# A softmax over rows of 512: transfers merged into one queue, the Tile context closed early, ScalarE in loops

## The chip, the core and the metric

The kernel runs on one core of one Trainium2 chip. The metric is device time in microseconds (us) of one execution; the profile, taken in an execution of its own, gives a span from the first to the last instruction and what every engine and every DMA queue did in it. Engines are called DVE (VectorE), ACT (ScalarE), POOL (GpSimd), PE (TensorE, unused here) and SP (SyncE). The 16 DMA engines move data between HBM and the on-chip memory; instructions issue transfers into queues, here the hardware queue of SP (q1 in the profile) and that of ACT (q10).

## The reference

```python
x = np.random.randn(16, 1024, 512).astype(np.float32)

def reference(x):
    x_max = np.max(x, axis=-1, keepdims=True)
    exp_x = np.exp(x - x_max)
    return (exp_x / np.sum(exp_x, axis=-1, keepdims=True)).astype(np.float32)
```

A softmax along the last axis: 16384 rows of 512 float32 values, 33.55 MB in and 33.55 MB out.

## The kernel before

The 16384 rows are cut into 8 chunks of 2048 rows. A chunk lies on 128 partitions with 16 rows on each (`CHUNK`), so a partition's part of a chunk is 32 KB that are contiguous in HBM too, and a chunk is 4.19 MB. The on-chip tile `held` has room for 6 chunks (`PLACES`); chunk k uses place k mod 6, and everything is computed in place. Chunks 6 and 7 therefore can be loaded only when chunks 0 and 1 have been stored.

The computation goes by groups of 8 rows a partition (`GROUP`), two groups to a chunk, 16 groups in all. For a group:

- `rowmax` (line 89): one DVE instruction gives the negated maximum of each row, `shift`.
- `exps` (line 94): eight ACT activations, one for each row of a partition, give exp(x + shift) in place; each also accumulates the row's sum into `sums`, which appears in the profile as a separate ACTIVATION_READ_ACCUMULATOR.
- `scale` (line 105): one small DVE instruction gives the reciprocals of the eight sums. Then, for groups 0 to 12 (`ON_POOL = 13`), one POOL instruction (line 107) multiplies the whole group of 4096 elements a partition with the reciprocals, which are broadcast along the row; for groups 13 to 15 eight DVE instructions (line 114) do it, one for each row.

The order on each engine is the program's order (`manual_schedule`): DVE does the maximum of group g ahead of the reciprocal of group g - 1. The Tile context supplies the semaphores between engines.

All loads are issued by SP (line 72): six at once at the beginning, the first of them ahead of the opening barrier of the program (`loads_at_the_head`). All stores are issued by ACT (line 75), between its activations; `STORE_BEHIND` says how many groups later a finished chunk's store stands in ACT's order. The loads of chunks 6 and 7 follow the stores of chunks 0 and 1 in the program; SP waits for those stores to land. So loads are in SP's queue and stores in ACT's.

When the Tile context ends (line 161), SP waits for every transfer and every engine's last instruction; then two barriers of all engines follow, with a clearing of the context's semaphores between them.

Of the kernel before, what the change touches and what calls it, by code (L numbers as in the profile page):

```python
# [1 line left out]

# [4 lines left out]

F32 = mybir.dt.float32
EXP = mybir.ActivationFunctionType.Exp
AX = mybir.AxisListType.X  # L10


CHUNK = 16
CHUNKS = 8
PLACES = 6
GROUP = 8

STORE_BEHIND = [1, 1, 1, 1, 0, 0, 0, 0]

LOAD_AFTER = {0: 6, 1: 7}  # L20
ON_POOL = 13


AT_HEAD = {mybir.EngineType.SP: 1}

def loads_at_the_head(nc):

    main, body = nc.main_func.blocks[0], nc.main_func.blocks[1]  # L30
    for engine, count in AT_HEAD.items():
        loads = [
            i
            for i in body.instructions
            if i.engine == engine and type(i).__name__ == "InstDMACopy"
        ][:count]
        barrier = next(
            n
            for n, i in enumerate(main.instructions)
            if i.engine == engine and type(i).__name__ == "InstDrain"  # L40
        )
        for load in loads:
            body.instructions.remove(load)
        main.instructions[barrier:barrier] = loads


@with_exitstack
def kernel(
    ctx: ExitStack,
    tc: tile.TileContext,  # L50
    x: bass.AP,
    out: bass.AP,
):
    nc = tc.nc
    nc.at_finalize(loads_at_the_head)
    P = nc.NUM_PARTITIONS

    x_rows = x.flatten_outer_dims().rearrange("(c p r) d -> c p r d", p=P, r=CHUNK)
    out_rows = out.flatten_outer_dims().rearrange("(c p r) d -> c p r d", p=P, r=CHUNK)
    n, _, _, d = x_rows.shape  # L60
    assert n == CHUNKS

    data = ctx.enter_context(tc.tile_pool(name="data", bufs=1))
    stats = ctx.enter_context(tc.tile_pool(name="stats", bufs=6))
    held = data.tile([P, PLACES * CHUNK, d], F32, name="held")

    def place(k):
        at = (k % PLACES) * CHUNK
        return held[:, at : at + CHUNK, :]

    def load(k):
        nc.sync.dma_start(out=place(k), in_=x_rows[k])  # L72

    def store(k):
        nc.scalar.dma_start(out=out_rows[k], in_=place(k))
        if k in LOAD_AFTER:
            load(LOAD_AFTER[k])

    per = CHUNK // GROUP
    groups = CHUNKS * per  # L80
    shift, sums = [None] * groups, [None] * groups

    def rows(g):
        at = (g % per) * GROUP
        return place(g // per)[:, at : at + GROUP, :]

    def rowmax(g):
        shift[g] = stats.tile([P, GROUP], F32, name="shift", tag="shift")
        nc.vector.reduce_max(out=shift[g], in_=rows(g), axis=AX, negate=True)  # L89

    def exps(g):
        sums[g] = stats.tile([P, GROUP], F32, name="sums", tag="sums")
        for r in range(GROUP):
            nc.scalar.activation(  # L94
                out=rows(g)[:, r, :],
                in_=rows(g)[:, r, :],
                func=EXP,
                bias=shift[g][:, r : r + 1],
                scale=1.0,
                accum_out=sums[g][:, r : r + 1],  # L100
            )

    def scale(g):
        recip = stats.tile([P, GROUP], F32, name="recip", tag="recip")
        nc.vector.reciprocal(out=recip, in_=sums[g])  # L105
        if g < ON_POOL:
            nc.gpsimd.tensor_mul(  # L107
                out=rows(g),
                in0=rows(g),
                in1=recip.unsqueeze(2).to_broadcast([P, GROUP, d]),  # L110
            )
            return
        for r in range(GROUP):
            nc.vector.tensor_scalar_mul(  # L114
                out=rows(g)[:, r, :],
                in0=rows(g)[:, r, :],
                scalar1=recip[:, r : r + 1],
            )

    with tc.manual_schedule():  # L120
        for k in range(PLACES):
            load(k)
        stored = 0
        for g in range(groups):
            rowmax(g)
            exps(g)
            if g:
                scale(g - 1)
            if stored < CHUNKS and g > (stored + 1) * per - 1 + STORE_BEHIND[stored]:
                store(stored)  # L130
                stored += 1
        scale(groups - 1)
        while stored < CHUNKS:
            store(stored)
            stored += 1


# [1 line left out]
_INS = ['x']  # L139
_OUTS = [((16, 1024, 512), 'float32')]  # L140


# [23 lines left out]
```

## Time and profile before

| What | Value |
|---|---|
| time, median of 3 runs | 161.96 us (161.58 to 162.31) |
| span of the profiled execution | 160.4 us |
| DVE, ACT, POOL busy | 51%, 58%, 57% of the span |
| DMA | 67.13 MB, mean 419 GB/s |

The profiled execution has no other time than its span. The median of the runs is 1.55 us longer than that span: the runs' time also holds what lies ahead of the first and behind the last instruction of the program.

How the views are read. The page's first rows give the busy time of each engine, its share and the number of instructions; the row "DMA" cuts the span into 40 slices and gives the mean busy share of the 16 DMA engines in tenths. The chain of waits follows the work that ended last backwards from one releaser to the next; its rows are start, duration, what. Groups of instructions give line, engine, operation, shapes and count, then busy time and mean duration in ns, then the idle time ahead of them and what ended it. The view by stretches gives, for each stretch, its length, the busy time and the number of instructions of DVE, ACT and POOL, the granted TensorE clock, the busy share of the DMA engines, and GB/s; bytes are counted where their packet begins. In the timeline an engine's name with a q (ACTq, SPq) is its sequencer: issues, waits and drains, which are not counted as busy.

### The profile page before, as it was taken

Reading aid. Unit: us, or ns where it says so; the run is one execution under the profiler, and the core shown is the slowest. Engines: PE = TensorE matmul, PEld = TensorE weight load, DVE = VectorE, ACT = ScalarE, POOL = GpSimd, SP = SyncE. Lnnn points to the kernel's source line nnn. Section 1 sums busy time; section 2 is a strip of 40 time slices with the busy share of each in tenths; the row PEclk is TensorE's granted clock in tenths of the full one; section 3 lists DMA queues with packets and bytes.
Section 4 is the critical chain, followed back from the end, with each engine's and each line's share of the span. In section 5 each row is a group of like instructions: output and inputs, shape, how many; then the busy total and the mean of one; then the engine's idle time right before and its main releaser. Section 6 shows DMA issues by size and latency. Waiting matters only on the chain.

```text
span 160.4 us, 425 instructions
## 1 busy us (share of the span) xinstructions
DVE 82.0 (51%) x56; ACT 92.7 (58%) x257; POOL 91.0 (57%) x17
## 2 busy tenths in 40 slices
DVE  0009967977977700893009920099202999671000
ACT  0003899999998996079900959409594195920000
POOL 0000039999999999999993899508995000000000
DMA  7999999999899999999999999999999999999993
GB/s 261 482 433 392 466 449 392 443 458 400 343 433 400 449 449 409 425 474 409 425 466 409 409 490 409 402 466 441 400 449 449 409 425 474 411 409 474 425 392 139
DMA packets 2307, 67.13 MB, mean 419 GB/s; under 512 B 256, under 2 KB 256, under 8 KB 256
## 3 DMA queue, kind: packets, MB, share of 16 engines
q1 hardware_dynamic: 1152, 33.55, 49.5%
q10 hardware_dynamic: 1152, 33.55, 48.5%
q14 instruction: 3, 0.02, 0.0%
HBM read 33.55 MB, written 33.55 MB: 418 GB/s over the span
## 4 chain that ended last, share of the span: by engine, by line
DMA 53%; POOL 14%; DVE 10%; ACT 7%; issue 7%; DVEq 0%; SPq 0%
DMA held<-in_x_dram 34%; DMA out_dram<-held 19%; POOL held L107 14%; ACT held L94 7%; DVE shift L89 6%; DVE held L114 4%; DVE recip L105 0%; DVEq L161 0%; SPq L72 0%; DVEq L105 0%; DVEq L89 0%
## 5 line engine op out<-in xcount | busy, mean ns | idle before, releaser
L94 ACT ACTIVATE held<-held,shift 128x512 f32<-128x512 f32 x128 | 90.6, 719 | 36.4 <-DVE shift L89 32.0
L107 POOL TENSOR_TENSOR held<-held,recip 128x4096 f32<-128x4096 f32 x13 | 90.8, 7018 | 31.5 <-DVE recip L105 31.5
L89 DVE TENSOR_REDUCE shift<-held 128x8 f32<-128x4096 f32 x16 | 70.2, 4393 | 46.9 <-DMA held<-in_x_dram 46.9
L94 ACT ACTIVATION_READ_ACCUMULATOR held<-held,shift 128x1 f32 x128 | 25.3, 198 | 0.0
L105 DVE RECIPROCAL recip<-sums 128x8 f32<-128x8 f32 x16 | 3.2, 200 | 16.0 <-ACT held L94 16.0
L114 DVE TENSOR_SCALAR held<-held,recip 128x512 f32<-128x512 f32 x24 | 9.8, 483 | 0.1
L94 ACT ACT_TABLE_LOAD x1 | 1.3, 1283 | 12.3 <-DMA held<-in_x_dram 12.3
L150 POOL MEMSET const-float32-0.0<- 128x1 f32 x1 | 0.1, 99 | 0.2 <-issue 0.2
L150 POOL MEMSET const-bfloat16-1.0<- 128x1 bf16 x1 | 0.1, 102 | 0.0
L150 POOL MEMSET const-uint8-127<- 128x1 uint8 x1 | 0.1, 102 | 0.0
L150 POOL MEMSET const-float32-1.0<- 128x1 f32 x1 | 0.1, 99 | 0.0
## 6 DMA issues: line engine op xcount, KB each, us to landing
held<-in_x_dram SPq DMA_DIRECT2D x8, 4096.0 KB, 41.8
out_dram<-held ACTq DMA_DIRECT2D x8, 4096.0 KB, 28.0
```

What stands on the lines that cost most here:

```text
L89: nc.vector.reduce_max(out=shift[g], in_=rows(g), axis=AX, negate=True)
L94: nc.scalar.activation(out=rows(g)[:, r, :], in_=rows(g)[:, r, :], func=EXP, bias=shift[g][:, r : r + 1], scale=1.0, accum_out=sums[g][:, ...
L105: nc.vector.reciprocal(out=recip, in_=sums[g])
L107: nc.gpsimd.tensor_mul(out=rows(g), in0=rows(g), in1=recip.unsqueeze(2).to_broadcast([P, GROUP, d]),)
L114: nc.vector.tensor_scalar_mul(out=rows(g)[:, r, :], in0=rows(g)[:, r, :], scalar1=recip[:, r : r + 1],)
L150: nc = _bacc.Bacc("TRN2", target_bir_lowering=False, num_devices=1)
```

## The change

The kernel after computes the same values in the same chunks and groups. What is different:

- **Own memory and semaphores.** `held`, `shift`, `sums` and `recip` are allocated directly, the three statistics with a place for every row, and the kernel declares its own semaphores: one for each load, one for each store, one for each chunk's finished multiplications, and four between the engines. `take` waits until a semaphore has reached n and lowers it by n.
- **Tile context closed early.** Only the six first loads stand in the context. It is closed behind them, so its closing barriers come right after the loads' issue. Nothing of the kind stands at the end; there SP waits for the six stores that no load has waited for.
- **One queue.** Stores are issued by SP too. After the six loads SP's order is: store 0, store 1, load 6, store 2, load 7, store 3 to 7, each store behind the wait for its chunk's two multiplications, loads 6 and 7 behind the landing of stores 0 and 1.
- **ScalarE in loops.** ACT loads its function table at once. Its 16 groups run in two loops, of 12 and of 4 turns, with eight activations in the body; the addresses of the rows and of the statistics are computed from the loop's counter in registers, by two instructions ahead of each activation.
- **Multiplications.** Groups 0 to 11 are multiplied on POOL as before, groups 12 to 15 on DVE (`ON_VECTOR`), there with the same single instruction with broadcast reciprocals in place of eight. Group 12 thus moves from POOL to DVE.
- The order on DVE is as before, with waits of its own: the maximum of a chunk's first group waits for its load, the reciprocal for ACT's group. The first POOL instruction that sets up the multiplication stands behind POOL's first wait; before, it stood ahead of it.

```diff
+ORDER = [("L", k) for k in range(PLACES)] + [
+    ("S", 0), ("S", 1), ("L", 6), ("S", 2), ("L", 7),
+    ("S", 3), ("S", 4), ("S", 5), ("S", 6), ("S", 7),
+]
+ON_VECTOR = (12, 13, 14, 15)
...
+    def take(engine, semaphore, n):
+        engine.wait_ge(semaphore, n).then_inc(semaphore, -n)
...
-    def load(k):
-        nc.sync.dma_start(out=place(k), in_=x_rows[k])
-
-    def store(k):
-        nc.scalar.dma_start(out=out_rows[k], in_=place(k))
-        if k in LOAD_AFTER:
-            load(LOAD_AFTER[k])
...
+    with tc.manual_schedule():
+        for _, k in ORDER[:PLACES]:
+            first = nc.sync.dma_start(out=place(k), in_=x_rows[k])
+            first.then_inc(loaded[k], 16)
+            tc.no_tile_sem_insts.add(first.ins.name)
+    tc.close()
+    tc.compile()
+
+    reused = set()
+    for what, k in ORDER[PLACES:]:
+        if what == "L":
+            if k >= PLACES:
+                take(nc.sync, stored[k - PLACES], 16)
+                reused.add(k - PLACES)
+            nc.sync.dma_start(out=place(k), in_=x_rows[k]).then_inc(loaded[k], 16)
+        else:
+            take(nc.sync, scaled[k], PER)
+            nc.sync.dma_start(out=out_rows[k], in_=place(k)).then_inc(stored[k], 16)
...
     def rowmax(g):
+        if g % PER == 0:
+            take(nc.vector, loaded[g // PER], 16)
+        nc.vector.reduce_max(
+            out=stats(shift, g), in_=rows(g), axis=AX, negate=True
+        ).then_inc(maxed, 1)
 
     def scale(g):
-        nc.vector.reciprocal(out=recip, in_=sums[g])
-        if g < ON_POOL:
-            nc.gpsimd.tensor_mul(...)
-            return
-        for r in range(GROUP):
-            nc.vector.tensor_scalar_mul(...)
+        engine, ready = (
+            (nc.vector, to_vector) if g in ON_VECTOR else (nc.gpsimd, to_pool)
+        )
+        take(nc.vector, expd, 1)
+        nc.vector.reciprocal(out=stats(recip, g), in_=stats(sums, g)).then_inc(ready, 1)
+        take(engine, ready, 1)
+        engine.tensor_mul(
+            out=rows(g),
+            in0=rows(g),
+            in1=stats(recip, g).unsqueeze(2).to_broadcast([P, GROUP, d]),
+        ).then_inc(scaled[g // PER], 1)
...
+    nc.scalar.preload_act_table(EXP)
+
+    def exps(first, turns):
+        with nc.scalar.Fori(0, turns) as i:
+            take(nc.scalar, maxed, 1)
+            for r in range(GROUP):
+                row = held[:, bass.ds(i * GROUP + r, 1), :]
+                at = bass.ds(i * GROUP + (first * GROUP + r), 1)
+                act = nc.scalar.activation(
+                    out=row, in_=row, func=EXP, bias=shift[:, at],
+                    scale=1.0, accum_out=sums[:, at],
+                )
+            act.then_inc(expd, 1)
+
+    exps(0, RING)
+    exps(RING, GROUPS - RING)
+
+    for k in range(CHUNKS):
+        if k not in reused:
+            take(nc.sync, stored[k], 16)
```

More of the change, by code (lines that the diff above doesn't have):

```diff
@@ L61 @@
     assert n == CHUNKS
-    data = ctx.enter_context(tc.tile_pool(name="data", bufs=1))
-    stats = ctx.enter_context(tc.tile_pool(name="stats", bufs=6))
-    held = data.tile([P, PLACES * CHUNK, d], F32, name="held")
+    held = nc.alloc_sbuf_tensor("held", [P, PLACES * CHUNK, d], F32).ap()
+    shift = nc.alloc_sbuf_tensor("shift", [P, GROUPS * GROUP], F32).ap()
+    sums = nc.alloc_sbuf_tensor("sums", [P, GROUPS * GROUP], F32).ap()
+    recip = nc.alloc_sbuf_tensor("recip", [P, GROUPS * GROUP], F32).ap()
+    loaded = [nc.alloc_semaphore(f"loaded{k}") for k in range(CHUNKS)]
+    stored = [nc.alloc_semaphore(f"stored{k}") for k in range(CHUNKS)]
+    maxed = nc.alloc_semaphore("maxed")
+    expd = nc.alloc_semaphore("expd")
+    to_pool = nc.alloc_semaphore("to_pool")
+    to_vector = nc.alloc_semaphore("to_vector")
+    scaled = [nc.alloc_semaphore(f"scaled{k}") for k in range(CHUNKS)]
+    def take(engine, semaphore, n):
+        engine.wait_ge(semaphore, n).then_inc(semaphore, -n)
     def place(k):
@@ L69, in place @@
         return held[:, at : at + CHUNK, :]
-    def load(k):
-        nc.sync.dma_start(out=place(k), in_=x_rows[k])
-    def store(k):
-        nc.scalar.dma_start(out=out_rows[k], in_=place(k))
-        if k in LOAD_AFTER:
-            load(LOAD_AFTER[k])
-    per = CHUNK // GROUP
-    groups = CHUNKS * per
-    shift, sums = [None] * groups, [None] * groups
-    def rows(g):
-        at = (g % per) * GROUP
-        return place(g // per)[:, at : at + GROUP, :]
-    def rowmax(g):
-        shift[g] = stats.tile([P, GROUP], F32, name="shift", tag="shift")
-        nc.vector.reduce_max(out=shift[g], in_=rows(g), axis=AX, negate=True)
@@ L91, in exps @@
-    def exps(g):
-        sums[g] = stats.tile([P, GROUP], F32, name="sums", tag="sums")
-        for r in range(GROUP):
[L94 to L101, printed above, removed]
-    def scale(g):
-        recip = stats.tile([P, GROUP], F32, name="recip", tag="recip")
-        nc.vector.reciprocal(out=recip, in_=sums[g])
-        if g < ON_POOL:
[L107 to L111, printed above, removed]
-            return
[L113 to L135, printed above, removed]
+    def rows(g):
+        at = (g % RING) * GROUP
+        return held[:, at : at + GROUP, :]
@@ new lines, in stats @@
+    def stats(t, g):
+        return t[:, g * GROUP : (g + 1) * GROUP]
+    with tc.manual_schedule():
[15 more added lines that the diff above has]
+            nc.sync.dma_start(out=out_rows[k], in_=place(k)).then_inc(stored[k], 16)
@@ new lines @@
+    for g in range(GROUPS):
+        rowmax(g)
+        if g:
+            scale(g - 1)
+    scale(GROUPS - 1)
+    nc.scalar.preload_act_table(EXP)
[6 more added lines that the diff above has]
+                act = nc.scalar.activation(
+                    out=row,
+                    in_=row,
+                    func=EXP,
+                    bias=shift[:, at],
+                    scale=1.0,
+                    accum_out=sums[:, at],
+                )
+            act.then_inc(expd, 1)
```

16 lines of the change are left out of this document (13 added, 3 removed).

## The prediction

> **What bounds the kernel now.** I read the page's shares first, to see whether an engine is full.
>
> ```profile
> span 160.4 us, 425 instructions
> ...
> DVE 82.0 (51%) x56; ACT 92.7 (58%) x257; POOL 91.0 (57%) x17
> ...
> DMA  7999999999899999999999999999999999999993
> ...
> q14 instruction: 3, 0.02, 0.0%
> HBM read 33.55 MB, written 33.55 MB: 418 GB/s over the span
> ```
>
> No engine works for 60% of the span, while the row of the DMA engines stands at 9 in nearly every slice. The kernel moves 67.1 MB, so the question is where it is not moving them at full rate. For that I cut the span into stretches, with the DMA engines' share and their GB/s as the last two columns.
>
> ```profile
> 0.00:12.25 12.25, 0.00 (x0) 0.00 (x0) 0.20 (x4) 1.00 0.94 385
> 12.25:36.00 23.75, 19.89 (x8) 20.56 (x56) 13.20 (x2) 1.00 1.01 438
> 36.00:44.00 8.00, 6.80 (x3) 8.00 (x23) 8.00 (x3) 1.00 0.95 352
> 44.00:157.00 113.00, 55.31 (x46) 64.16 (x180) 69.60 (x10) 1.00 1.01 434
> 157.00:157.60 0.60, 0.00 (x0) 0.00 (x0) 0.00 (x0) 1.00 0.38 164
> 157.60:158.50 0.90, 0.00 (x0) 0.00 (x0) 0.00 (x0) 1.00 0.09 36
> 158.50:160.40 1.90, 0.00 (x0) 0.00 (x0) 0.00 (x0) 1.00 0.00 0
> ```
>
> The plateau is 434 GB/s for 113 us. It is the same while loads and stores share the engines, up to 122, and when only stores are left:
>
> ```profile
> 81.00:122.00 41.00, 18.04 (x8) 23.05 (x64) 31.89 (x5) 1.00 1.01 434
> 122.00:157.00 35.00, 18.95 (x29) 11.53 (x32) 0.71 (x1) 1.00 1.00 433
> ```
>
> At that rate 67.1 MB take 154.6 us. The remaining 5.8 us of the span lie in four places:
>
> - the start: 385 GB/s x 12.25 us = 4.72 MB, worth 10.9 us, so 1.4 us lost;
> - a dip at 36 to 44: with the stretch ahead of it, 31.75 us move 10.40 + 2.82 = 13.22 MB, worth 30.5 us, so 1.3 us lost;
> - the end of the transfers: 164 x 0.6 + 36 x 0.9 = 0.13 MB, worth 0.3 us, in the 2.7 us from 157.0 to the last landing, so 2.4 us lost. One packet alone begins after 157.6 (36 GB/s x 0.9 us is 32 KB): one DMA engine is some 0.8 us behind the others;
> - what follows the landing.
>
> The landing is read from SyncE's drains of the Tile context, the first of which stands behind its waits for all stores:
>
> ```profile
> L161 SPq EVENT_SEMAPHORE  x7: 17/28/28, 120.2 to 160.3; - x7
> ...
> L161 SPq DRAIN  x3: 7/7/7, 159.7 to 160.0; - x3
> ```
>
> From 159.7 to the end at 160.4 stand only the two closing barriers: 0.7 us. The sum is 154.6 + 1.4 + 1.3 + 2.4 + 0.7 = 160.4, the span. The chain of waits that ended last agrees:
>
> ```profile
> 0.00 12.25 DMA held<-in_x_dram
> ...
> 16.73 5.77 ACT held L94 x16
> ...
> 50.78 30.72 DMA out_dram<-held
> ...
> 81.57 41.80 DMA held<-in_x_dram
> ```
>
> Its middle runs over a store that takes 30.7 us and a load that takes 41.8 us from issue to landing: transfers stand in line behind each other, in two queues. (Its second row shows eight activations with their accumulator reads, one group, in 5.77 us.)
>
> **The change part by part.**
>
> *Context closed early.* The two closing barriers go behind the sixth load's issue. They cost the end 0.7 us now; I keep 0.1 for SyncE's last wait. At the start they stand behind the issue of six loads:
>
> ```profile
> 0.00 3.17 SPq L72 DMA_DIRECT2D held<-in_x_dram  x6
> ```
>
> They are over near 3.2 + 0.7 = 3.9 us, and every engine's first work waits for the load that lands at 12.25: 8 us of cover.
>
> *One queue.* The order of transfers becomes L0 to L5, S0, S1, L6, S2, L7, S3 to S7 (L load, S store). With 4.19 MB at 434 GB/s each takes 9.66 us, and the n-th lands at 12.25 + 9.66(n - 1): L5 at 60.5, S0 70.2, S1 79.9, L6 89.5, S2 99.2, L7 108.9, S3 118.5, S4 128.2, S5 137.8, S6 147.5, S7 157.2. A hole appears only if a transfer is issued after its predecessor landed. L6 waits for S0 and holds up S2 behind it in SyncE's queue, but S1 is in flight for 9.7 us then; L7 waits for S1 while L6 and S2 are queued. So no wait of SyncE empties the queue if the computation meets the landing times.
>
> ```profile
> 22.80 13.99 POOL L107 TENSOR_TENSOR held<-held,recip 128x4096 f32<-128x4096 f32 x2 [22.37 <-DVE recip L105]
> ...
> L107 POOL TENSOR_TENSOR held<-held,recip 128x4096 f32<-128x4096 f32 x13 | 90.8, 7018 | 31.5 <-DVE recip L105 31.5
> L89 DVE TENSOR_REDUCE shift<-held 128x8 f32<-128x4096 f32 x16 | 70.2, 4393 | 46.9 <-DMA held<-in_x_dram 46.9
> ...
> L105 DVE RECIPROCAL recip<-sums 128x8 f32<-128x8 f32 x16 | 3.2, 200 | 16.0 <-ACT held L94 16.0
> L114 DVE TENSOR_SCALAR held<-held,recip 128x512 f32<-128x512 f32 x24 | 9.8, 483 | 0.1
> ```
>
> GpSimd's first two groups end at 22.8 + 14.0 = 36.8, S0 is due at 60.5. Its twelve groups end at 22.8 + 12 x 7.02 = 107.0 if fed without a gap, S5 is due at 128.2. One wait moves: group 13's reciprocal and multiplication stand on VectorE behind the maximum of group 14, which waits for L7. So S6 is ready at 108.9 + 4.4 + 0.2 + 4.4 = 117.9 and due at 137.8. S7 then follows: maximum 15 to 122.3, reciprocal and multiplication 14 to 126.9, the exponentials of group 15 to 128.1, and 0.2 + 4.4 more make 132.7; due at 147.5. The smallest cover is 14.8 us. Now the last store is issued late and is still in time:
>
> ```profile
> 145.03 0.34 ACTq L75 DMA_DIRECT2D out_dram<-held  x1
> ```
>
> What the single queue does to the dip is not shown by any row. At best the dip belongs to the second queue's start at the first store (the row of the issue at 36.83 is below, the dip begins there): 0. At worst the first writes cost the same 1.3 us again. Beyond that the queue turns between loads and stores five times; each turn lies between 0 (both directions alternate at 434 GB/s from 44 on) and 1.3 us. I take 0.5 us for all five, close to the plateau's row, since the alternating traffic there loses nothing.
>
> *The end of the transfers.* The late engine's 0.8 us: besides the data only queue 14 uses the engines, with three packets of 8 KB of instructions. ScalarE's 128 written-out activations become two loops of eight, so its stream shrinks and there should be fewer such packets. Bounds: 0.8 gained, 0 gained; I take 0.6 gained, so 1.8 us remain of 2.4.
>
> *ScalarE in loops.* Each activation gets two register instructions ahead of it, each turn a branch. No row prices them. The nearest is a DMA issue, also sequencer work:
>
> ```profile
> 36.50 0.73 ACT L94 ACTIVATE held<-held,shift 128x512 f32<-128x512 f32 x1
> 36.83 0.38 ACTq L75 DMA_DIRECT2D out_dram<-held  x1
> ...
> 37.21 0.73 ACT L94 ACTIVATE held<-held,shift 128x512 f32<-128x512 f32 x1
> ```
>
> It takes 0.38 us and the next activation still starts 0.71 us after the last, so up to that much is hidden. Bounds: 0 (hidden), or 0.38 us exposed per activation: 16 groups x (5.77 + 3.04) from 16.7 end at 157.7, and the end breaks. The cover is (147.5 - 4.6 - 16.7)/16 - 5.77 = 2.1 us a group, 0.26 us an activation. I take 0.
>
> *Broadcast multiplications on VectorE*, for groups 12 to 15: one instruction over 4096 elements in place of eight of 0.48 us. Bounds 3.3 us (the eight, overlapped) and GpSimd's 7.02; I took 4.4 above, the maximum's row over as many elements. At 7.02 the three on S7's way (13, 14, 15) bring it from 132.7 to 139.4, still 8.1 us early: 0. The same cover takes the table load that no longer waits for L0 and GpSimd's configuration, now behind its first wait (S0 has 23.7 us).
>
> The sum: 154.6 + 1.4 + 0.5 + 1.8 + 0.1 = 158.4 us of span. The profile's page gives no time for this execution but its span; the median of the runs, 161.96, lies 1.55 above it, and I add the same: 159.95, so **160.0 us**, 1.2% faster.
>
> **The rivals.**
>
> *Only the barriers go.* The dip and the late engine stay: 154.6 + 1.4 + 1.3 + 2.4 + 0.1 = 159.8, with 1.55 it is 161.3. For it: the dip begins where the first store begins, and any first store may cost it. Against: the dip is in no later start of a store. [...]
>
> *Every turn of the queue costs.* Within one queue a store behind a load might not overlap with it. At the dip's 1.3 us for each of five turns: 154.6 + 1.4 + 6.5 + 1.8 + 0.1 = 164.4, with 1.55 it is 166.0. It decides from (160.4 - 157.9)/5 = 0.5 us a turn on. For it: loads and stores follow each other in one queue nowhere in the trace before. Against: from 44 to 122 directions alternate, and nothing is lost.
>
> *The loops cost.* Past 0.26 us an activation the last store is late; at the 0.38 us bound group 15's exponentials end at 157.7; 4.6 of reciprocal and multiplication and a transfer's 12.25 from issue to landing (the first load's) make a span of 174.6, 176.1 with what lies around. Against: the row of 0.38 us hidden. [...]
>
> **How the numbers follow.** Forecast 0.66 (158.6 to 161.0), only the barriers 0.18 (161.0 to 162.0), turns 0.09, loops 0.05, anything else slower 0.02. About 0.5%, 0.8 us, is what a measurement of this kernel can tell from no change; faster is below 161.15. The forecast and 0.03 from the barrier case's lower edge give 0.69 faster; the rest of that case and 0.01 of cheap turns give 0.16 for same; 0.15 is left for slower. Low: dip 0, lateness 0.8 gained, no last wait: 157.6 + 1.55 = 159.1, and 0.5 for what lies around the span, which the early end of the other engines may shorten: 158.6. High: the barrier case's 161.3 with half a dip, 0.65, for the other turns: 162.0.
>
> **What would show it.** In the profile after: the span ends within 0.1 us of the last landing; one hardware queue carries 67 MB; no stretch after the start falls below 420 GB/s at 36 to 44, and a dip at 60 would give the rival its 1.3 us; queue 14 has fewer packets; the last store is issued near 133. I am wrong if stretches around the five turns lie under 434, if the last store is issued after 147, or if queue 14 has more packets than 3.

## The result and the profile after

| | before | after |
|---|---|---|
| time, median | 161.94 us (161.52 to 162.93, 6 runs) | 160.43 us (160.17 to 160.92, 6 runs) |
| ratio to before | | 0.990, 95% interval 0.987 to 0.993 |
| span of the profiled execution | 160.4 us | 159.1 us (its own time: 160.39) |

The kernel is faster by 1.0%. The forecast was 160.0 (158.6 to 162.0), with the kernel faster by 1.2%. Runs of the kernel before that lie more than 1.5% above its fastest (5 of 29 beside the first experiments, 2 of 11 beside the others) are left out of the medians and ratios below.

The first rows of the page after, as they answer to those before:

```profile
span 159.1 us, 740 instructions
...
DVE 95.0 (60%) x36; ACT 92.0 (58%) x257; POOL 83.9 (53%) x16
...
q1 hardware_dynamic: 2304, 67.11, 98.9%
q14 instruction: 2, 0.02, 0.0%
```

All 67.11 MB are in SP's queue, and queue 14 moved two instruction packets instead of three. VectorE is busier by 13 us: it multiplies group 12 as well, where, as is seen below, the multiplication took 9.46 us, and for groups 13 to 15 the single instruction takes 4.42 us where the eight took 3.3.

The view by stretches, with the DMA engines' share and GB/s as the last two columns:

```profile
0.00:12.25 12.25, 0.00 (x0) 1.28 (x1) 0.20 (x4) 1.00 0.95 385
12.25:36.00 23.75, 19.58 (x8) 18.96 (x53) 12.61 (x2) 1.00 1.02 439
36.00:44.00 8.00, 6.92 (x3) 8.00 (x25) 8.00 (x2) 1.00 0.93 401
44.00:55.00 11.00, 8.75 (x5) 11.00 (x31) 11.00 (x3) 1.00 1.02 438
55.00:65.00 10.00, 7.77 (x5) 10.00 (x30) 10.00 (x2) 1.00 1.03 410
65.00:157.00 92.00, 52.01 (x19) 42.76 (x122) 42.13 (x7) 1.00 1.00 432
157.00:157.60 0.60, 0.00 (x0) 0.00 (x0) 0.00 (x0) 1.00 0.63 273
157.60:158.50 0.90, 0.00 (x0) 0.00 (x0) 0.00 (x0) 1.00 0.01 0
```

Two readings. No data packet begins after 157.6 any more: the engine that was late before is not late here. And a low rate alone does not make a dip, because bytes are counted where a packet begins, and the packets of the 16 engines, 32 KB each, begin close together, within 0.5 us of each round of 1.21 us (from 36.74 to 37.23, say, by the trace's list of packets): 36 to 44 shows 401 GB/s only because part of such a volley falls outside. A measure without that edge is the mean time of a packet, 16 engines x 32.77 KB x share / rate, so 524.3 x share / rate in us. At the plateau it is 524.3 x 1.00 / 432 = 1.21 us; in 36 to 44 it is 524.3 x 0.93 / 401 = 1.22, no dip; in 55 to 65 it is 524.3 x 1.03 / 410 = 1.32. Before, 36 to 44 had 524.3 x 0.95 / 352 = 1.41. Shorter stretches, the first of the kernel before, the other two of the kernel after, show where the slow packets are:

```profile
38.00:41.50 3.50, 2.34 (x3) 3.50 (x12) 3.50 (x1) 1.00 1.14 365
```

```profile
57.00:60.00 3.00, 3.00 (x1) 3.00 (x10) 3.00 (x2) 1.00 1.09 350
...
87.00:90.00 3.00, 0.00 (x0) 0.00 (x0) 3.00 (x1) 1.00 1.01 415
```

The mean packet takes 1.64 us there before and 1.63 after. So the slow packets did not go away. They moved from the first store's place in time before to its place after, the end of load 5. A weaker dip, of 1.28 us a packet, lies at 87 to 90, ahead of store 2.

The end of the program, from SyncE's waits (with the start of the first and of the last) and from the timeline of its issues of load 6, load 7 and store 7, where each row begins with the start:

```profile
L94 SPq EVENT_SEMAPHORE  x16: 17/17/17, 37.4 to 159.0; - x16
```

```profile
71.29 0.34 SPq L124 DMA_DIRECT2D held<-in_x_dram  x1
```

```profile
81.36 0.34 SPq L124 DMA_DIRECT2D held<-in_x_dram  x1
```

```profile
135.82 0.33 SPq L127 DMA_DIRECT2D out_dram<-held  x1
```

The last wait, for store 7, passes at 159.0 and the span ends at 159.1; before, 0.7 us of barriers stood there. Loads 6 and 7 are issued the moment stores 0 and 1 have landed, so those landed near 71.3 and 81.4. The last store is issued at 135.8, some 12 us before the 147.5 at which its predecessor was forecast to land.

### The profile page after: what moved, and what is told of

It is laid out like the page before. It is cut to its first block, busy times and chain, and to the rows that moved or that the text cites. A ratio compares the mean times of both kernels' runs of the same rounds, so it can differ in the third digit from the quotient of the medians.

```text
span 159.1 us, 740 instructions
## 1 busy us (share of the span) xinstructions
DVE 95.0 (60%) x36; ACT 92.0 (58%) x257; POOL 83.9 (53%) x16
## 3 DMA queue, kind: packets, MB, share of 16 engines
q1 hardware_dynamic: 2304, 67.11, 98.9%
## 5 line engine op out<-in xcount | busy, mean ns | idle before, releaser
L165 ACT ACTIVATE held<-held,shift x128 | 90.3, 713 | 34.9 <-ACTq L94 34.9
L144 POOL TENSOR_TENSOR held<-held,recip 128x4096 f32<-128x4096 f32 x12 | 83.7, 7017 | 23.0 <-POOLq L94 23.0
L165 ACT ACTIVATION_READ_ACCUMULATOR held<-held,shift x128 | 24.7, 193 | 0.0
L144 DVE TENSOR_TENSOR held<-held,recip 128x4096 f32<-128x4096 f32 x4 | 22.7, 5684 | 0.6
## 6 DMA issues: line engine op xcount, KB each, us to landing
out_dram<-held SPq DMA_DIRECT2D x8, 4096.0 KB, 31.2
```

Of the source, the lines that this page charges most:

```text
L144: engine.tensor_mul(out=rows(g), in0=rows(g), in1=stats(recip, g).unsqueeze(2).to_broadcast([P, GROUP, d]),).then_inc(scaled[g // PER], 1)
L165: act = nc.scalar.activation(out=row, in_=row, func=EXP, bias=shift[:, at], scale=1.0, accum_out=sums[:, at],)
```

## The experiments

Every run below is the changed kernel with one edit, except where it says otherwise. Ratios are to the kernel before, run beside the same experiments; beside the first four it had a median of 161.98 us over 24 runs, with a span of 160.2 (median). The changed kernel itself was run again beside the first four only. Its two medians, 160.43 and 160.24, differ by 0.19 us, so smaller differences between runs that did not stand side by side tell nothing.

**The changed kernel again**, as a yardstick for its neighbours.

> The changed kernel once more, as the yardstick for the runs beside it. Both theories: 160.2 to 160.6 us, 0.99 of the kernel before, last landing within 0.1 us of the end of the span.

160.24 us (160.08 to 160.55, 6 runs), ratio 0.988 (0.984 to 0.992). Its median span is 158.9, so 1.35 us lie outside it; of the kernel before, 1.79 us lie outside (median of the differences in its 24 runs). The gain of 1.74 us is thus 1.3 inside the span and 0.45 outside.

**Two barriers put back at the end.**

```diff
     for k in range(CHUNKS):
         if k not in reused:
             take(nc.sync, stored[k], 16)
+    nc.all_engine_barrier()
+    nc.all_engine_barrier()
```

> Two barriers of all engines are put back at the end of the changed kernel. Theory (the barriers stood on the path, and their 0.7 us were half of the gain): the span is 0.5 to 0.8 us longer than the changed kernel's and the time 160.9 to 161.2. Rival (what lies behind the program's last instruction waits for all engines anyway, so the runs' time does not feel them): the span grows, the time stays at 160.4 within 0.2.

161.24 us (161.03 to 161.54, 12 runs), ratio 0.995 (0.992 to 0.997). That is 1.0 us above the yardstick: its median span is 159.45, 0.55 longer, and 1.79 us lie outside, 0.44 more, as in the kernel before. The rows of its profile:

```profile
L94 SPq EVENT_SEMAPHORE  x16: 17/17/17, 37.5 to 158.8; - x16
```

```profile
L184 POOLq EVENT_SEMAPHORE  x2: 17/17/17, 159.3 to 159.4; - x2
```

Store 7 landed at 158.8, earlier than in the changed kernel's profile, and the second barrier ran until the span's end at 159.5. So the barriers are worth 1.0 us: the theory holds, with more than it expected. The part outside the span was in neither theory. That engines which are let go early finish their closing work earlier, and that this is what shortens it, is the author's estimate; no run shows it.

**The first six loads in ACT's queue.**

```diff
-            first = nc.sync.dma_start(out=place(k), in_=x_rows[k])
+            first = nc.scalar.dma_start(out=place(k), in_=x_rows[k])
...
-AT_HEAD = {mybir.EngineType.SP: 1}
+AT_HEAD = {mybir.EngineType.Activation: 1}
```

> The first six loads go into ACT's queue, everything else stays in SP's: two queues again, all else as in the changed kernel. Theory (the engines work at the same rate from one queue or two, and the dip belongs to the first store): the dip moves back to where the first store is issued, 36 to 44, and is as deep as before, some 1 us; the time is 160.4 within 0.3. Rival (the merging is what gained the other half, 0.6 us): 160.9 to 161.3.

161.40 us (159.98 to 161.88, 12 runs), ratio 0.995 (0.992 to 0.997). The stretches that matter:

```profile
36.00:44.00 8.00, 6.91 (x3) 8.00 (x23) 8.00 (x2) 1.00 1.01 393
...
157.60:158.50 0.90, 0.00 (x0) 0.00 (x0) 0.00 (x0) 1.00 0.01 0
158.50:160.20 1.70, 0.00 (x0) 0.00 (x0) 0.00 (x0) 1.00 0.04 19
```

The slow packets are back at 36 to 44 (524.3 x 1.01 / 393 = 1.35 us), as the theory had it. But the time is at the rival's, 0.1 above its range: one packet (19 GB/s x 1.7 us = 32 KB) begins after 158.5, when all other engines are done. One engine is late again, and by more than a packet's 1.21 us.

**ScalarE's loops written out.**

```diff
-        with nc.scalar.Fori(0, turns) as i:
+        for i in range(turns):
             take(nc.scalar, maxed, 1)
...
```

Behind these lines the rows are addressed by number instead of by register.

> The two loops on ScalarE are written out as 128 activations, all else as in the changed kernel. Theory (fetched instructions hold up single DMA engines, and fewer of them is what made the end of the transfers earlier): queue 14 moves 3 packets or more instead of 2, and one engine's last packet begins 0.3 to 0.8 us behind the others', time 160.7 to 161.2. Rival (the packets do not matter for the end): 160.4 within 0.2. Both: ScalarE's activations keep 0.71 us each, since the register instructions were hidden.

161.68 us (160.04 to 162.13, 12 runs), ratio 0.995 (0.992 to 0.999): the theory's side, but 0.5 us above its range. Queue 14 and the end:

```profile
q14 instruction: 3, 0.02, 0.0%
```

```profile
157.60:158.50 0.90, 0.00 (x0) 0.00 (x0) 0.00 (x0) 1.00 0.09 36
158.50:160.40 1.90, 0.00 (x0) 0.00 (x0) 0.00 (x0) 1.00 0.04 17
```

One packet begins in each of the two stretches: one engine is some two packets behind. The activations take 706 ns on average here and 713 in loops, so the register instructions were hidden as forecast.

**Store 0 ahead of load 5.**

```diff
-ORDER = [("L", k) for k in range(PLACES)] + [
+ORDER = [("L", k) for k in range(PLACES - 1)] + [
     ("S", 0),
+    ("L", PLACES - 1),
     ("S", 1),
...
```

Load 5 is no longer issued in the Tile context, which holds five loads.

> In SP's order store 0 stands ahead of load 5 instead of behind it; the first store is then the sixth transfer. Theory (the packets ahead of the first store run slower, wherever it stands): the slow packets come one transfer earlier, near 48 to 51 instead of 58 to 61, and the stretch 36 to 55 is the one that falls below 434 GB/s; time 160.3 within 0.3. Rival (the dip is due to what happens at that time, such as VectorE, ScalarE and GpSimd working together): it stays at 58 to 61.

160.13 us (160.03 to 160.16, 4 runs), ratio 0.985 (0.977 to 0.992).

```profile
44.00:55.00 11.00, 8.76 (x5) 11.00 (x33) 11.00 (x3) 1.00 1.05 420
55.00:65.00 10.00, 7.77 (x5) 10.00 (x29) 10.00 (x2) 1.00 0.99 429
```

The mean packet takes 1.31 us in 44 to 55 and 1.21 in 55 to 65: the slow packets went with the first store. The order also has two turns between loads and stores more than the changed kernel, and its time is not above that kernel's.

**A small store ahead of everything, from ACT's queue**, of zeros into rows of chunk 0. The text of the edit, with store 0 waiting for `warmed`:

```diff
...
+    nc.vector.memset(warm, 0.0).then_inc(warm_set, 1)
+    take(nc.scalar, warm_set, 1)
+    nc.scalar.dma_start(out=out_rows[0][:, 0:1, :], in_=warm).then_inc(warmed, 16)
...
```

> A small store (128 x 2 KB of zeros, into rows of chunk 0 that store 0 writes again later) is issued from ACT's queue near 4 us. Theory (the dip is a price of the first write to the output): no dip at 58 to 61; the loads around 5 us are slower instead, by as much, so the time stays at 160.3 within 0.4. Rival (the price belongs to the first large store or to the first turn in SP's queue): the dip of some 0.7 us stays at 58 to 61.

160.76 us (160.68 to 161.14, 4 runs). In 55 to 65 the share is 0.96 at 370 GB/s, a mean packet of 1.36 us: the dip stayed, as the rival of this run had it, and the time is 0.3 to 0.5 us above the changed kernel's two medians besides.

**A small copy from input to output as ACT's first instruction.**

```diff
+        warm = nc.scalar.dma_start(
+            out=out_rows[0][:, 0:1, 0:128], in_=x_rows[0][:, 0:1, 0:128]
+        )
...
-AT_HEAD = {mybir.EngineType.SP: 1}
+AT_HEAD = {mybir.EngineType.Activation: 1, mybir.EngineType.SP: 1}
```

> A small copy of 128 x 512 bytes from the input to rows of chunk 0 of the output (overwritten later by store 0) is the very first instruction of ACT, beside the first load's start. Theory (the price belongs to the first write to the output, and beside the first load's own start it costs little): no dip at 58 to 61, last landing 0.3 to 0.8 us earlier, time 159.5 to 160.0. Rival (the price belongs to the first transfer out of the on-chip memory): the dip stays, time 160.3 within 0.2 or up to 0.5 later.

160.47 us (160.19 to 161.03, 6 runs); 55 to 65 has 1.03 at 419 GB/s, 1.29 us a packet. Writing to the output early does not take the dip away, so it is not a price of the first write to that memory. The time is the rival's, but the cause that the rival names, the first transfer out of the on-chip memory, does not fit the run before, where a small transfer of that kind came near 5 us and the dip stayed.

**A small store in SP's own queue, behind load 3** (the small store of zeros from above, issued by SP).

> A small store of 128 x 2 KB of zeros stands in SP's own queue behind load 3, into rows that store 0 writes later. Theory (the slow packets belong to the first store in a queue that has run loads only): the slow packets come near 38 to 41, and the stretch 55 to 65 keeps 430 GB/s or more. Rival (only a store of full packets does it): the stretch 55 to 65 stays near 410.

A single run, 160.62 us:

```profile
36.00:44.00 8.00, 6.93 (x3) 8.00 (x25) 8.00 (x2) 1.00 1.00 426
...
55.00:65.00 10.00, 7.77 (x5) 10.00 (x29) 10.00 (x2) 1.00 1.00 410
```

The mean packet takes 1.28 us in 55 to 65 and 1.23 in 36 to 44. The dip stayed with the first large store, so the rival of this run holds.

**Eight scalar multiplications on VectorE again**, for groups 12 to 15.

```diff
+        if engine is nc.vector:
+            for r in range(GROUP):
+                row = rows(g)[:, r, :]
+                mul = nc.vector.tensor_scalar_mul(
+                    out=row, in0=row, scalar1=stats(recip, g)[:, r : r + 1]
+                )
+            mul.then_inc(scaled[g // PER], 1)
+            return
```

> Groups 12 to 15 are multiplied on VectorE by eight instructions with a scalar operand each, as before the change, instead of one with two tensors. Theory (the broadcast multiplication of group 12 took 9.46 us because it waited for GpSimd's last one, and both forms are hidden): the multiplication of group 12 takes 3.3 to 4 us if this form does not need what GpSimd holds, the last store is issued 5 to 9 us earlier than at 135.8, and the time is 160.3 within 0.3. Rival: the scalar form waits for GpSimd too, the first of its instructions taking 5 us or more.

160.32 us (159.94 to 160.49, 4 runs), ratio 0.986 (0.978 to 0.994): the form makes no difference to the time. The last store was issued at 132.9, 2.9 us earlier than in the changed kernel and not the 5 to 9 of the theory. The timeline of VectorE in the changed kernel, GpSimd's last multiplications in it, and VectorE's in this run:

```profile
101.95 9.46 DVE L144 TENSOR_TENSOR held<-held,recip 128x4096 f32<-128x4096 f32 x1
111.33 4.41 DVE L133 TENSOR_REDUCE shift<-held 128x8 f32<-128x4096 f32 x1
115.66 0.18 DVE L142 RECIPROCAL recip<-sums 128x8 f32<-128x8 f32 x1
115.99 4.42 DVE L144 TENSOR_TENSOR held<-held,recip 128x4096 f32<-128x4096 f32 x1
```

```profile
93.14 13.99 POOL L144 TENSOR_TENSOR held<-held,recip 128x4096 f32<-128x4096 f32 x2
```

```profile
101.80 8.69 DVE L147 TENSOR_SCALAR held<-held,recip 128x512 f32<-128x512 f32 x8
...
115.39 3.26 DVE L147 TENSOR_SCALAR held<-held,recip 128x512 f32<-128x512 f32 x8
```

GpSimd's last multiplication ends at 93.14 + 13.99 = 107.13. VectorE's first begins at 101.95 and ends 4.28 us after GpSimd, where it takes 4.42 with GpSimd idle: it took 5 us longer, and what lies behind GpSimd's end is close to a whole multiplication. The scalar form does the same, 8.69 us against 3.26, with 3.05 us of it behind GpSimd's end at 107.44 in that run. So the rival of this run holds in size: both forms took some 5 us longer beside GpSimd. That they wait for it is what these times suggest; no row shows what they wait for.

**First six loads in ACT's queue and loops written out**, both edits from above.

> Both at once: the six first loads in ACT's queue and the activations written out. Each alone cost 1.2 and 1.4 us. Theory (each only makes one DMA engine late, and the end waits for the latest engine, so the two do not add up): 161.3 to 162.0 us. Rival (two losses that are independent of each other): 162.6 to 163.0.

160.93 us (160.06 to 161.60, 6 runs), ratio 0.989 (0.983 to 0.995): below the theory's range, and far from a sum of 1.2 and 1.4 us. The two edits together are no worse than either alone.

**Shorter instruction streams.**

```diff
-ON_VECTOR = (12, 13, 14, 15)
+ON_VECTOR = ()
+HALF = GROUP // 2
...
-        ).then_inc(maxed, 1)
+        ).then_inc(maxed, 2)
...
-        with nc.scalar.Fori(0, turns) as i:
+        with nc.scalar.Fori(0, 2 * turns) as i:
...
-            for r in range(GROUP):
+            for r in range(HALF):
...
```

> The changed kernel with shorter instruction streams: ScalarE's loop bodies have four activations instead of eight (with twice the turns), and GpSimd multiplies all 16 groups, so VectorE has four multiplications and four waits less. Theory (a fetched instruction packet makes one DMA engine late): queue 14 moves 0 or 1 packets inside the span instead of 2, the stretch behind 157 ends 0.2 to 0.6 us earlier, time 159.7 to 160.1. Rival (the spread at the end has other causes): 160.2 to 160.4 with fewer packets.

160.35 us (160.14 to 161.63, 6 runs), ratio 0.988 (0.982 to 0.994), with one packet in queue 14. The theory's gain did not come; the time is the rival's. GpSimd now does all 16 multiplications, and that is hidden too.

**Short streams and store 0 ahead of load 5.**

> The short streams together with store 0 ahead of load 5, which has two turns between loads and stores more than the changed kernel. Theory (turns cost nothing but the first): as the short streams alone within 0.2 us, 159.6 to 160.1. Rival (each turn costs something): 0.3 us or more above the short streams alone.

160.41 us (160.17 to 162.09, 6 runs), ratio 0.989 (0.983 to 0.996), 0.06 above the short streams alone: that is within the theory's 0.2, though above its 159.6 to 160.1, and the two turns more cost nothing that these runs show. No run is clearly faster than the changed kernel; the lowest median, 160.13, is from four runs.

## Why the prediction was right

**The bound.** The forecast rests on the DMA engines being full and everything else hidden. That held: the engines' busy share was 1.00 from 65 to 157, VectorE's multiplications in either form, or on GpSimd, leave the time where it was (160.32 and 160.35 us), and activations in loops or written out both take 0.71 us with their addressing hidden.

**The sum, term by term**, from the stretches after:

| term | forecast | measured |
|---|---|---|
| 67.1 MB at 434 GB/s | 154.6 | 154.6 |
| start, to 12.25 | 1.4 | 1.4 (385 GB/s again) |
| dip and turns, 12.25 to 157 | 0.5 | 0.8 to 65, and 0.4 after (92 us at 432 instead of 434) |
| end of the transfers | 1.8 | 1.7 (2.04 us from 157.0 to 159.04, less 0.16 MB, worth 0.4) |
| behind the last landing | 0.1 | below 0.1 |
| outside the span | 1.55 | 1.3 |

(0.8: the stretches from 12.25 to 65 move 10.43 + 3.21 + 4.82 + 4.10 = 22.56 MB, worth 52.0 of 52.75 us. The measured terms make a span of 158.9, which rounding of the rates separates from 159.1.) Two terms were mis-sized: the dip and the turns came out 0.7 us larger, what lies outside the span 0.25 smaller. They partly cancel, and so much of the agreement is luck. What gained inside the span can be seen in the two profiles: the last data packet ends at 158.56 instead of 159.22, and the 0.7 us of barriers behind it are gone.

**The signs that the prediction named.** The span ends with the last landing, SP's queue carries 67.11 MB, queue 14 moves two packets, and the last store is issued at 135.8 where 133 was said. One sign of being wrong came up: the stretch around the first turn, 55 to 65, runs at 410 GB/s and not at 434. What it hits is the term of the dip; at 0.8 us instead of 0.5 that is too little to carry the time out of the range. The 401 GB/s at 36 to 44, below the 420 that was named, are the edge effect shown above.

**The dip** was taken at 0.5 between 0 and 1.3, on the thought that the second queue's start might be its cause. By the mean time of its packets the dip before cost 1.1 us and not the 1.3 that the bytes gave (352 x 8.00 / 524.3 = 5.4 packets an engine, each 0.2 us longer). The slow packets followed the first store through every order tried, with one queue or two, and neither an early write to the output nor a small store in either queue removed them. The turns after the first are not quite free, as the forecast had nearly assumed: ahead of store 2 the mean packet takes 1.28 us from 87 to 90. But two turns more cost nothing that the times show, so the rival that charges each turn a full dip falls.

**The barriers** were counted as 0.6 us of span; put back, they cost 0.55 there, and 0.44 outside the span. The forecast carried the 1.55 us outside over unchanged, and that step failed in size. It had also been read from a profiled span against the median of other runs, where the runs' own spans give 1.79. The rival in which only the barriers go forecast 161.3; its own mechanism, at its measured 1.0 us, gives 161.0 from 161.98.

**The late engine.** 0.6 of 0.8 us was taken as gained by fewer instruction packets, and the term came out in size (1.7 against 1.8). The changed kernel's profile shows no late engine. Both undoings bring one back in most runs: the first loads in ACT's queue with two instruction packets, as many as the changed kernel has, the written-out activations with three. Undone together they cost no more, and a packet fewer gained nothing.

What the late engines carried can be followed in the trace's list of DMA packets. In the profile before, a packet begins within 0.01 us of the end of its engine's last one, and each engine closes its eight data packets of a transfer with one of 4 bytes (2048 of 32 KB and 256 of 4 bytes for 16 transfers and 16 engines), so the packets can be strung into one chain for each engine. The engine that ended last there, at 159.2 where the next ended at 158.4, had carried two of the three instruction packets (31.2 and 100.6 us). Each took 0.31 us, and the data packets behind these two took 0.32 and 0.25 us longer than the usual 1.21: 1.2 us together. With the activations written out the last engine had again two of three (37.2 and 76.9 us), 1.1 us together. In the profile after, the two packets (100.8 and 126.4 us) fell on two engines that were not behind the others: they ended at 158.2 and 158.5, the last engine at 158.56. So the mechanism of the step is right, instruction packets did make an engine late, but what counted was that two fell on the same engine, and not their number alone. They are not the only cause either: with the loads in ACT's queue the last engine had one instruction packet (101.9 us, 0.55 us) and three slow data packets ahead of stores 2 and 3 (1.0 us), and with both edits undone two slow data packets there (1.3 us). Each of these is one profile. What decides on which engine a packet falls, and so in which run an engine falls behind, stays open.

**The one queue.** At the plateau one queue and two carry the same: 432 GB/s with one, 434 with two before. The times are not the same: with the loads in ACT's queue, ten of twelve runs are above 161.2 us, and none of the changed kernel's is above 160.92. Why an engine falls behind more often with two queues is open.

**The cover.** S7 was to be ready at 132.7 and was issued at 135.8, with 147.5 as its due time. VectorE's multiplication was bounded by GpSimd's 7.02 us, and the first took 9.46, beside GpSimd's, where with GpSimd idle it takes 4.42. The bound failed because it priced each engine's instruction alone. That is not the whole 3.1 us: load 7 landed at 110.4 and not at 108.9, and the maximum that waits for it began only at 111.33, behind the 9.46 us. Of the cover of 14.8 us 11.7 were left. The loops cost 74 ns and 35 ns (medians, in the first loop) of register instructions for an activation, ahead of the engine:

```profile
L165 ACTq FUSED_REGOPS  x160: 42/74/88, 16.8 to 126.7; - x160
L165 ACT ACTIVATE held<-held,shift x128: 704/713/724, 17.0 to 130.0; - x128
...
L165 ACTq ALU_OP  x96: 35/35/35, 16.9 to 80.0; - x96
```

The loops' turns end in 16 branch instructions of 40 to 45 ns, 14 of which go back (12 and 4 turns), and two instruction packets are all that moved in the span.

## What to carry to other kernels

When the transfers fill the span, look at its two ends and at the slowest DMA engine: closing barriers behind the last landing cost 1.0 us here, of which only 0.55 can be seen inside the span. Compare whole spans with whole times, run by run, before carrying the difference over. Follow the engine that ends last back through its packets, since what one engine lost was not made up here (1.8 us behind at 121.4 and at the end, with the activations written out). And judge a dip by the mean time of its packets, not by its GB/s, since packets are counted where they begin.

## What the runs showed of the hardware

- The last one or two packets of each engine ahead of the first large store ran slower (a mean of 1.64 us from 38 to 41.5 in the profile before and of 1.63 from 57 to 60 in the profile after, instead of 1.21; 1.31 over the whole of 44 to 55 with store 0 ahead of load 5), wherever that store stood in the orders tried; ahead of store 2 a weaker dip (1.28 us from 87 to 90) is left. Why is open; an early write to the output and an earlier small store in either queue did not take it away.
- Each engine moved eight data packets of each of these transfers (2048 of 32 KB in 16 transfers, on 16 engines). An instruction packet of 8 KB took 0.31 us of a DMA engine in all five cases of the profiles before and after, and the data packet behind it was 0.11 to 0.35 us longer in the cases followed. The written-out activations' last engine, 1.8 us behind the next at 121.4, was still 1.8 us behind at the end.
- VectorE's multiplication with two tensors took 9.46 us (101.95 to 111.41) where GpSimd multiplied until 107.13, and 4.42 to 4.43 with GpSimd idle; with a tensor and a scalar, eight instructions took 8.69 us beside GpSimd and 3.26 with it idle. What makes them slower is not shown.
- Outside the span 1.79 us lie with closing barriers (medians of 24 and 12 runs) and 1.30 to 1.35 without, in every set of runs.
